# Attention 2: the low score pass as pairs of 64-row matmuls

## The chip, the core and the metric

The kernel runs on one core of one Trainium2 chip. The metric is device time in microseconds (us), the median of several runs. The engines are TensorE (PE in the profile, its weight loads PEld), VectorE (DVE), ScalarE (ACT), GpSimd (POOL) and SyncE (SP, which issues most transfers).

## What is computed

A trunk of two layers over 1024 frames of width 1024. Layer 1 mixes tokens by latent attention, layer 2 by differential attention; after each comes a SwiGLU block, and every step ends in a layer norm. The change concerns layer 2. Each of its 8 heads has two softmax maps of head width 64:

```python
logits = jnp.einsum('bqhmd,bkhmd->bmhqk', q_b, k) * scale
logits = logits - slopes[:, None, None] * dist
logits = jnp.where(_chunk_mask(i * Q_BLOCK, s), logits, NEG_BIG)
p = jax.nn.softmax(logits, axis=-1)
a = p[:, 0] - lam * p[:, 1]
o = jnp.einsum('bhqk,bkhe->bqhe', a, v)
```

The mask is causal over chunks of 64 frames, so a block of 128 queries with number i (0 to 7) sees (i + 1) * 128 keys.

## The kernel before, in words

Values in fp32 are split in two parts, a high part rounded to fp32r and a low part that is the rest, and a product is made of three matmuls: high by high, high by low, low by high. A tile planner orders the instructions of each engine ahead of time, by its own estimate of when operands and buffers are ready; at run time every engine works through its list in that order. `behind(i, j)` (line 167) tells the planner to keep instruction i after j.

**Attention 2** (from line 1263) works head by head. `proj_b` (line 1300) makes the queries and keys of a head, for half of the sequence at a time. A query tile `q2` has 1024 columns, 512 for each map; rows 0 to 63 and rows 64 to 127 both hold the map's high queries (a transfer copies them from one half of the partitions to the other). The keys `kt` hold, for map m, the high keys in the 64 rows from 64 * m and the low keys in the other 64. One matmul of 128 rows on `q2` and the keys so gives high by high plus high by low. The low queries `ql` of map m lie in the 64 rows from 64 * m, beside the high keys of that map; the other 64 rows are zero, so that a second matmul of 128 rows adds low by high alone. The zeros are written once: `store_zeros` (line 1233, in attention 1, slot 14) copies zeros to a tile and stores them to `zero_dr` (line 964), and six transfers at lines 1276 to 1279 load them into the three `ql` buffers. One of these three buffers is half of a tile that the profile calls `bq`; the other two are `ql`.

`score_b` (line 1329) scores one block of queries of one head: for each map it calls `softmax_block` (line 218). That takes the keys in one part up to 512 keys, else in two halves (widths 128, 256, 384, 512, then twice 320, 384, 448, 512). For each part it takes one PSUM bank of the group `s` (three of them in attention 2: `PS_BUFS_B`, line 38), runs the two matmuls into it (line 228), and lets VectorE add the bias, write the logits to SBUF and keep the extreme value (line 231, tiles `l_b` and `mx_b`). ScalarE then makes the exponentials with their sum (line 234), and VectorE the sum's reciprocal `r_b` (line 236). When both maps are done, GpSimd scales map 1 (line 1341), and VectorE combines the two (line 1342).

`attention` (line 270) sets the order: blocks are scored two ahead of the block that is transposed (`transpose_block`, tiles `pt_b`) and multiplied with the values (`pv_group`, tiles `o_b`); scores have the highest priority. The projections of the next head (`bp`), its values (`bv`), and the norms of finished heads (`norm_b2`, line 1368, which takes banks of the group `s` too) are put into numbered slots between the blocks.

Of the kernel before, what the change touches and what calls it, by code (L numbers as in the profile page):

```python
# [9 lines left out]
F32 = mybir.dt.float32  # L10
F32R = mybir.dt.float32r
AF = mybir.ActivationFunctionType
ALU = mybir.AluOpType
# [3 lines left out]
P = 128  # L17
# [17 lines left out]
BIGF = 3.0e38  # L35
# [7 lines left out]
def trunk(  # L43
# [32 lines left out]
    nc = tc.nc  # L76
    V, A, G, T = nc.vector, nc.scalar, nc.gpsimd, nc.tensor
# [9 lines left out]
    wp = ctx.enter_context(tc.tile_pool(name="wp", bufs=3))  # L87
# [12 lines left out]
    dr = ctx.enter_context(tc.tile_pool(name="dr", bufs=1, space=DRAM))  # L100
# [7 lines left out]
    def f32(t):  # L108
        return t.bitcast(F32)
# [4 lines left out]
    def ps_s(name):  # L114
        return ps.tile([P, 512], F32, tag="s", bufs=ps_bufs[0], name=name)
# [17 lines left out]
    def small(name, n=1):  # L133
        return sp.tile([P, 2], F32, tag="small", name=name, bufs=22)[:, :n]
# [32 lines left out]
    def behind(i, j):  # L167

        tc.add_manual_dep(
            i, j.name,  # L170
            mybir.DependencyInfo(mybir.DependencyClass.NoSync, mybir.DependencyReason.DATA),
            reason="kept in program order",
        )
# [44 lines left out]
    def softmax_block(lp, q_pass, s_bias, i, scale, name):  # L218
        n = (i + 1) * P
        nb = 1 if n <= 512 else 2  # L220
        w = n // nb
        l = lp.tile([P, 1024], F32, tag="l", name=f"l_{name}")
        mx = BIGF
        for b in range(nb):
            s = ps_s(f"s_{name}_{b}")
            ks = slice(b * w, (b + 1) * w)
            for j, (lh, rh) in enumerate(q_pass):
                T.matmul(s[:, :w], lh, rh[:, ks], start=(j == 0), stop=(j == len(q_pass) - 1))
            bv = s_bias[:, 896 - P * i + b * w:896 - P * i + (b + 1) * w]
            m = small(f"mx_{name}_{b}")  # L230
            V.tensor_tensor_reduce(l[:, ks], s[:, :w], bv, -scale, mx, ALU.add, ALU.min, m)  # L231
            mx = m
        sm = small(f"sm_{name}")
        newest["exp"] = A.activation(l[:, :n], l[:, :n], AF.Exp, bias=mx, scale=-1.0, accum_out=sm).ins  # L234
        r = small(f"r_{name}")
        V.reciprocal(r, sm)  # L236
        return l, r
# [32 lines left out]
    def attention(score, turn, mix, fill, la, hp):  # L270


        blocks = [(h, i) for h in range(H - 1) for i in range(NTB)] + [(H - 1, i) for i in LAST_ORDER]
        for fn in fill.get(-1, ()):
            fn()
        for b in range(la):
            score(*blocks[b])
        for b, (h, i) in enumerate(blocks):
            if b and i % 2 == 0:
                mix(blocks[b - 1][0], blocks[b - 1][1] // 2)  # L280
            if b + la < len(blocks):
                with tc.high_priority(hp[0]):
                    score(*blocks[b + la])
            with tc.high_priority(hp[1]):
                turn(h, i)
            for fn in fill.get(b, ()):
                fn()
        mix(blocks[-1][0], blocks[-1][1] // 2)
# [672 lines left out]
    spin(8, "spin0")  # L961

    o_dr = [[dr.tile([H, P, 256], F32, name=f"o_dr{l}_{g}") for g in range(4)] for l in range(2)]
    zero_dr = dr.tile([P, 512], F32, name="zero_dr")
    wo_dr = [dr.tile([P, 2, D], F32, name=f"wo_dr{h}") for h in range(H)]
    xs_dr = [dr.tile([S, D], F32, name=f"xs_dr{l}") for l in range(3)]

# [6 lines left out]
    ba, cos, sin = (krp.tile([P, S], F32, tag=t, name=t) for t in ("ba", "cos", "sin"))  # L974
# [130 lines left out]
    with ast as st:  # L1105
        pool = st.enter_context(tc.tile_pool(name="a1", bufs=2, reuse_waits="tile"))
        vp = st.enter_context(tc.tile_pool(name="a1v", bufs=12, side="right", reuse_waits="tile"))
        lp = st.enter_context(tc.tile_pool(name="a1l", bufs=4, side="right", reuse_waits="tile"))
# [97 lines left out]
        def at(slot, fn, *args):  # L1206
            fill.setdefault(slot, []).append(lambda: fn(*args))
# [9 lines left out]
        for h in range(1, H):  # L1217
            b = 8 * (h - 1)
# [11 lines left out]
        at(10, load_late)  # L1230
        at(12, make_late)

        def store_zeros():
            t = wp.tile([P, 1024], F32R, tag="wl", name="zeros")
            A.copy(t[:, :512], ba[:, :512])
            nc.sync.dma_start(zero_dr, f32(t[:, :512]))

        at(14, store_zeros)
        attention(score_a, turn_a, mix_a, fill, 2, (0, 0))

    banks("ps2", PS_BUFS)
# [22 lines left out]
    with ExitStack() as st:  # L1264
        lp = st.enter_context(tc.tile_pool(name="b1l", bufs=5, reuse_waits="tile"))
        pool = st.enter_context(tc.tile_pool(name="b1", bufs=2, reuse_waits="tile"))
        ptp = st.enter_context(tc.tile_pool(name="b1p", bufs=4, reuse_waits="tile"))
        bb = pool.tile([P, S], F32, tag="bb", name="bb", bufs=1)
# [4 lines left out]
        ob = big_tile("bo", F32)  # L1273
        q_hi = [qt[0][:, 0], qt[0][:, 1], qt[1][:, 0]]
        q_lo = [qt[1][:, 1]] + [pool.tile([P, S], F32R, tag=f"ql{j}", name=f"ql{j}", bufs=1) for j in range(2)]
        for ql in q_lo:
            for mp in range(2):
                b = slice(64 - mp * 64, 128 - mp * 64)
                nc.sync.dma_start(f32(ql[b, mp * 512:mp * 512 + 512]), zero_dr[b])

        def values_b(pr, tb):
            if ("v", pr) not in wts:
# [46 lines left out]
        def score_b(h, i):  # L1329
            c = slice((i % 4) * P, (i % 4) * P + P)  # L1330
            n = (i + 1) * P
            (q2, ql), k = q_slot[h, i // 4], kt[h % 2]
            (l0, r0), (l1, r1) = [
                softmax_block(
                    lp,
                    [(t[:, m * 512:m * 512 + 512][:, c], k[:, m]) for t in (q2, ql)],
                    bb, i, float(2.0 ** -(h + 1)), f"b{h}_{i}_{m}",
                )
                for m in range(2)
            ]  # L1340
            G.tensor_scalar(l1[:, :n], l1[:, :n], r1, nlam, ALU.mult, ALU.mult)  # L1341
            V.scalar_tensor_tensor(l0[:, :n], l0[:, :n], r0, l1[:, :n], ALU.mult, ALU.add)
            lt[h, i] = l0
# [67 lines left out]
        for h in range(1, H):  # L1411
            b = 8 * (h - 1)
# [20 lines left out]
        b = 8 * (H - 1) - 2  # L1433
        at(b - 1, begin_out)
        for slot, what, args in (
# [3 lines left out]
        ):  # L1439
            at(b + slot, lambda what, *a: getattr(proj[0], what)(*a), what, *args)  # L1440
        attention(score_b, turn_b, mix_b, fill, 2, (0, 60))
        norm_b(H - 1, 0, 2)
        norm_b2(H - 1, 0, 2)
# [94 lines left out]
```

## Time and profile before

| | |
|---|---|
| median of 3 runs | 2290.31 us (2287.85 to 2290.47) |
| the profiled execution | 2289.49 us |
| its span | 2287.7 us |
| granted clock of TensorE | 0.996 |
| first and last score of attention 2 | 1135.2 us, 1546.5 us |

The profile is of one execution. Times in its views are in microseconds from the start of the span, unless marked ns. "128*128 128x384" on a matmul is the size of the weights and of the result. A matmul's record runs from its start to a modelled end, and records of successive matmuls overlap; the time that a matmul takes of TensorE is read from the start of one to the start of the next. "idle before <- X" is the time in which an engine stood still before an instruction, and what it waited for.

### The profile page before, as it was taken

What the parts mean: (1) busy time and instruction counts of PE and PEld (TensorE: products, weight loads), DVE (VectorE), ACT (ScalarE), POOL (GpSimd) and SP (SyncE); (2) the same over time, 40 slices, a digit from 0 to 9 for tenths busy, and PEclk for the clock granted to TensorE, in tenths of its full rate; (3) what the DMA queues carried; (4) which work ended last, traced back from release to release, by engine and by line L of the source; (5) the groups of instructions that cost most, each with busy time, mean ns of one, the idle gap of its engine ahead of it and who ended that gap; (6) DMA issues with size and microseconds to landing.
All of it is one profiled execution on the core that took longest, in us unless ns stands there. A gap on an engine that the chain in (4) does not pass through costs nothing. (4 is left out here: it accounts for less than half of the span.)

```text
span 2287.7 us, 31159 instructions
## 1 busy us (share of the span) xinstructions
PE 2248.8 (98%) x11426; PEld 1916.5 (84%) x11426; DVE 1548.3 (68%) x2887; ACT 1019.3 (45%) x2101; POOL 871.6 (38%) x682
## 2 busy tenths in 40 slices
PE   9999999999999999999999999999999999999997
PEld 9888898888888887888888888987778888887886
DVE  6666765596666568667476666676586566657777
ACT  4465664352333334445465656555432233334353
POOL 2233452114444445555232424221014444436564
PEclk9999999999999999999999999999999999999999
DMA  6121325334313238554310212144344232337453
GB/s 205 41 94 56 123 97 184 135 141 141 126 69 138 73 117 328 187 185 166 107 47 24 65 38 70 37 194 129 120 161 157 69 123 85 122 129 306 141 203 123
DMA packets 104281, 289.33 MB, mean 126 GB/s; under 512 B 8640, under 2 KB 31808, under 8 KB 93632
## 3 DMA queue, kind: packets, MB, share of 16 engines
q1 hardware_dynamic: 100128, 277.90, 34.6%
q0 software_dynamic: 4000, 9.44, 1.4%
q8 instruction: 90, 1.47, 0.3%
q14 instruction: 63, 0.52, 0.1%
HBM read 205.78 MB, written 77.33 MB: 124 GB/s over the span
## 5 line engine op out<-in xcount | busy, mean ns | idle before, releaser
L513 ACT CAST op_g<-gr 128x512 fp32r<-128x512 f32 x240 | 147.5, 622 | 410.3 <-PE gb L557 227.7
L513 POOL TENSOR_TENSOR op_g<-gr,op_g 128x512 fp32r<-128x512 f32 x104 | 143.9, 1389 | 295.2 <-DVE tmp L650 154.0
L513 DVE TENSOR_TENSOR op_h<-rh,op_h 128x512 fp32r<-128x512 f32 x154 | 155.6, 1041 | 62.3 <-ACT op_h L513 62.3
L557 PE MATMUL ga<-xh_m,op_g 128*128 128x512 f32 x512 | 168.0, 389 | 0.0
L513 ACT CAST op_h<-rh 128x512 fp32r<-128x512 f32 x154 | 93.0, 620 | 155.3 <-PE dx L834 47.2
L834 PE MATMUL dw<-op_w_t,op_h 128*128 128x512 f32 x660 | 151.1, 390 | 0.0
L834 PEld LDWEIGHTS dw<-op_w_t,op_h 128*128 128x128 f32 x660 | 123.6, 188 | 25.7 <-DVE op_h L513 0.2
L234 ACT ACTIVATE l_b<-l_b,mx_b 128x256 f32<-128x256 f32 (+7 forms) x128 | 99.6, 778 | 78.4 <-DVE mx_b L231 75.5
L1341 POOL TENSOR_SCALAR l_b<-l_b,r_b,cst 128x128 f32<-128x128 f32 (+3 forms) x64 | 52.8, 825 | 205.9 <-DVE r_b L236 199.9
L834 PE MATMUL dx<-op_w_b,op_h 128*128 128x512 f32 x528 | 124.5, 397 | 5.3 <-DVE op_w_b L513 5.1
L513 POOL TENSOR_TENSOR op_w_t<-tt,op_w_t 128x512 fp32r<-128x512 f32 x66 | 98.4, 1493 | 79.7 <-ACT op_w_t L513 77.0
L834 PEld LDWEIGHTS dx<-op_w_b,op_h 128*128 128x128 f32 x528 | 101.1, 192 | 28.0 <-DVE op_w_b L513 6.0
L513 DVE TENSOR_TENSOR op_g<-gr,op_g 128x512 fp32r<-128x512 f32 x136 | 111.6, 822 | 9.5 <-ACT op_g L513 9.0
L557 PE MATMUL gb<-t4h_f,op_g 128*128 128x512 f32 x352 | 115.8, 390 | 0.6 <-DVE tmp L642 0.5
L557 PE MATMUL gc<-t1h_f,op_g 128*128 128x512 f32 x352 | 115.8, 389 | 0.5 <-ACT op_g L513 0.5
L557 PE MATMUL gb<-t3h_f,op_g 128*128 128x512 f32 x352 | 115.4, 389 | 0.7 <-ACT op_g L513 0.7
L557 PE MATMUL gc<-b22h_f,op_g 128*128 128x512 f32 x352 | 115.5, 389 | 0.0
L557 PE MATMUL gb<-t2h_f,op_g 128*128 128x512 f32 x352 | 114.8, 389 | 0.0
L557 PEld LDWEIGHTS ga<-xh_m,op_g 128*128 128x128 f32 x512 | 96.1, 188 | 20.0
L513 POOL TENSOR_TENSOR op_g<-s,op_g 128x512 fp32r<-128x512 f32 x40 | 55.4, 1385 | 149.2 <-ACT op_g L513 149.2
L155 PE MATMUL bp<-xT_f,h_wb 128*128 128x512 f32 x256 | 103.0, 402 | 0.0
L157 PE MATMUL bp<-xT_f,l_wb 128*128 128x512 f32 x256 | 101.6, 397 | 0.0
(376 smaller groups left out, 6751.8 us busy)
## 6 DMA issues: line engine op xcount, KB each, us to landing
gr<-in_w_gu SPq DMA_DIRECT2D x44, 1024.0 KB, 6.9
rh<-h_dr SPq DMA_DIRECT2D x28, 1024.0 KB, 5.3
h_dr<-sh SPq DMA_DIRECT2D x22, 1024.0 KB, 4.9
h_dr<-hp SPq DMA_DIRECT2D x22, 768.0 KB, 4.1
tt<-in_w_dn SPq DMA_DIRECT2D x22, 512.0 KB, 9.2
rh<-h_dr SPq DMA_DIRECT2D x14, 768.0 KB, 4.4
z<-xs_dr SPq DMA_DIRECT2D x16, 512.0 KB, 11.7
rw_b<-in_w_dn SPq DMA_DIRECT2D x8, 1024.0 KB, 8.3
```

What stands on the lines that cost most here:

```text
L155: T.matmul(ps_out, lh, rh, start=(i == 0), stop=False)
L157: T.matmul(ps_out, ll, rh, start=False, stop=(i == n - 1))
L234: newest["exp"] = A.activation(l[:, :n], l[:, :n], AF.Exp, bias=mx, scale=-1.0, accum_out=sm).ins
L513: return A.copy(hi, src).ins, eng.tensor_tensor(lo, src, f32(hi), ALU.subtract).ins
L557: T.matmul(o, w[:, a, kc], x[b][:, k, :], start=(first and k == 0 and (a, b) == (0, 0)), stop=(k == 3 and a == 1), skip_group_check=True,)
L834: T.matmul(o, h[:, a, c], w[:, b_], start=(first and (a, b_) == (0, 0)), stop=(last and a == 1), skip_group_check=True,)
L1341: G.tensor_scalar(l1[:, :n], l1[:, :n], r1, nlam, ALU.mult, ALU.mult)
```

## The change

`score_b` no longer calls `softmax_block`. For each part of the keys it takes two banks, one for each map, and issues the high matmuls of both maps (128 rows), then the low matmuls of both maps. A low matmul has 64 rows: those from 64 * m of the low queries and of the keys. A `behind` keeps the first low matmul after the second high one. VectorE's two reductions of the part follow, and when all parts are done, map 0's exponentials and reciprocal, then map 1's. The zeros are no longer needed: their copy, their store and their six loads are removed. What follows the softmax is unchanged.

```diff
-    zero_dr = dr.tile([P, 512], F32, name="zero_dr")
...
-        def store_zeros():
-            t = wp.tile([P, 1024], F32R, tag="wl", name="zeros")
-            A.copy(t[:, :512], ba[:, :512])
-            nc.sync.dma_start(zero_dr, f32(t[:, :512]))
-
-        at(14, store_zeros)
...
-        for ql in q_lo:
-            for mp in range(2):
-                b = slice(64 - mp * 64, 128 - mp * 64)
-                nc.sync.dma_start(f32(ql[b, mp * 512:mp * 512 + 512]), zero_dr[b])
...
             (q2, ql), k = q_slot[h, i // 4], kt[h % 2]
-            (l0, r0), (l1, r1) = [
-                softmax_block(
-                    lp,
-                    [(t[:, m * 512:m * 512 + 512][:, c], k[:, m]) for t in (q2, ql)],
-                    bb, i, float(2.0 ** -(h + 1)), f"b{h}_{i}_{m}",
-                )
-                for m in range(2)
-            ]
+            nb = 1 if n <= 512 else 2
+            w = n // nb
+            ls = [lp.tile([P, 1024], F32, tag="l", name=f"l_b{h}_{i}_{m}") for m in range(2)]
+            mx = [BIGF, BIGF]
+            for b in range(nb):
+                ks = slice(b * w, (b + 1) * w)
+                ss = [ps_s(f"s_b{h}_{i}_{m}_{b}") for m in range(2)]
+                pe = []
+                for t in (q2, ql):
+                    for m, s in enumerate(ss):
+                        a = slice(0, P) if t is q2 else slice(m * 64, m * 64 + 64)
+                        pe.append(T.matmul(
+                            s[:, :w], t[a, m * 512:m * 512 + 512][:, c], k[a, m, ks], start=(t is q2), stop=(t is ql),
+                            skip_group_check=True,
+                        ).ins)
+                behind(pe[2], pe[1])
+                bv = bb[:, 896 - P * i + b * w:896 - P * i + (b + 1) * w]
+                for m, s in enumerate(ss):
+                    x = small(f"mx_b{h}_{i}_{m}_{b}")
+                    V.tensor_tensor_reduce(
+                        ls[m][:, ks], s[:, :w], bv, -float(2.0 ** -(h + 1)), mx[m], ALU.add, ALU.min, x
+                    )
+                    mx[m] = x
+            rs = []
+            for m in range(2):
+                sm = small(f"sm_b{h}_{i}_{m}")
+                A.activation(ls[m][:, :n], ls[m][:, :n], AF.Exp, bias=mx[m], scale=-1.0, accum_out=sm)
+                r = small(f"r_b{h}_{i}_{m}")
+                V.reciprocal(r, sm)
+                rs.append(r)
+            (l0, l1), (r0, r1) = ls, rs
```

## Prediction

> **What bounds the kernel now.** I read the page's busy shares first, then the busy time of the second attention's stretch, then who waits there, and last the single matmuls in order of time.
>
> The page's first lines:
>
> ```profile
> span 2287.7 us, 31159 instructions
> ...
> PE 2248.8 (98%) x11426; PEld 1916.5 (84%) x11426; DVE 1548.3 (68%) x2887; ACT 1019.3 (45%) x2101; POOL 871.6 (38%) x682
> ```
>
> TensorE is busy for 98% of the span. Two stretches (start:end, length, then busy time and instructions of PE, PEld, DVE, ACT and POOL, the granted clock, DMA share, GB/s): that of the zeros' loads, and from the first score of attention 2 to nearly its end.
>
> ```profile
> 1068.00:1090.00 22.00, 22.00 (x123) 19.16 (x122) 15.09 (x30) 12.21 (x24) 7.43 (x5) 1.00 0.20 61
> 1135.00:1550.00 415.00, 411.35 (x2496) 363.98 (x2495) 283.25 (x847) 244.06 (x562) 131.70 (x126) 1.00 0.21 68
> ```
>
> In the second stretch TensorE is idle for 415.00 - 411.35 = 3.65 us, and VectorE, the next, is busy for 283 of 415. The waits of that stretch (who waits, for whom: total us, times, longest):
>
> ```profile
> DVE l_b L231 <- PE s_b L228: 23.0, 25, 4.1
> ...
> PE s_b L228 <- DVE mx_b L231: 1.5, 2, 1.1
> ```
>
> VectorE waits for scores more than TensorE waits for banks. A matmul that disappears here should therefore leave the span, as long as the row of work behind it can move up. Which matmuls are touched, by tile:
>
> ```profile
> L228 PE MATMUL s_b<-bk,bq x256: 220/358/741, 1135.2 to 1546.5; 128*128 128x384 f32 x32, 128*128 128x512 f32 x32, 128*128 128x320 f32 x20, 128*128 128x448 f32 x20
> L228 PE MATMUL s_b<-bk,ql x128: 272/340/486, 1150.1 to 1527.9; 128*128 128x384 f32 x32, 128*128 128x512 f32 x32, 128*128 128x320 f32 x24, 128*128 128x448 f32 x24
> ```
>
> Together 384, which is 96 groups of four: two maps, each with a high pass and a low pass. (One of the three low-query buffers lies in a bq tile, hence 256 and 128.) All are 128*128, full height. By the code a head has one group of width 128, one of 256, two of 320, three of 384, two of 448 and three of 512: 12 groups, times 8 heads.
>
> A matmul's record is longer than its place in the row, so I price by start to start. Runs of scores and what follows them:
>
> ```profile
> 1180.06 0.27 PE L228 MATMUL s_b<-bk,bq 128*128 128x128 f32 x1
> ...
> 1180.51 0.45 PE L155 MATMUL bp<-xT_f,h_wb 128*128 128x512 f32 x1
> ...
> 1260.35 0.33 PE L228 MATMUL s_b<-bk,bq 128*128 128x384 f32 x1
> ...
> 1261.04 0.39 PE L157 MATMUL bp<-xT_f,l_wb 128*128 128x512 f32 x1
> ...
> 1296.77 0.31 PE L228 MATMUL s_b<-bk,ql 128*128 128x320 f32 x1
> ...
> 1297.21 0.40 PE L156 MATMUL bp<-xT_f,h_wb 128*128 128x512 f32 x1
> ...
> 1337.19 0.28 PE L228 MATMUL s_b<-bk,bq 128*128 128x256 f32 x1
> ...
> 1337.67 0.27 PE L160 MATMUL pt_b<-ident,l_b 128*128 128x128 f32 x1
> ...
> 1343.20 0.40 PE L228 MATMUL s_b<-bk,ql 128*128 128x512 f32 x1
> 1343.43 0.39 PE L228 MATMUL s_b<-bk,bq 128*128 128x512 f32 x1
> ...
> 1343.89 0.27 PE L160 MATMUL pt_b<-ident,l_b 128*128 128x128 f32 x1
> ...
> 1425.62 0.36 PE L228 MATMUL s_b<-bk,ql 128*128 128x448 f32 x1
> 1425.82 0.36 PE L228 MATMUL s_b<-bk,bq 128*128 128x448 f32 x1
> ...
> 1426.63 0.39 PE L155 MATMUL bp<-xT_f,h_wb 128*128 128x512 f32 x1
> ```
>
> Four matmuls of 128 take 0.45 us, four of 384 0.69, three of 320 0.44, four of 256 0.48, three of 512 0.69, five of 448 1.01. One matmul's place s is then 0.1125, 0.1725, 0.147, 0.120, 0.230 and 0.202 us. Below 256 columns s falls no further: there the weight load sets the pace, so 0.1125 is one load's place. The loads of the last run:
>
> ```profile
> 1425.62 0.19 PEld L228 LDWEIGHTS s_b<-bk,bq 128*128 128x128 f32 x1
> 1425.82 0.19 PEld L228 LDWEIGHTS s_b<-bk,ql 128*128 128x128 f32 x1
> ```
>
> Each load starts just as the matmul ahead of its own starts (1425.62, 1425.82): one set of weights is prepared while another is in use.
>
> **The change part by part.**
>
> *The pair.* Each group's four matmuls stay four instructions with four loads, but the last two have 64 rows each, on the two halves of the array and into two banks. No row of this trace shows such a matmul. Its price lies between nothing beyond its neighbour (side by side) and its full place. I take side by side, because the halves share neither weights nor banks, and both are ready once the low queries are there. The loads I take one after the other, both from the start of the last high matmul, as the load rows suggest: 2 x 0.1125 = 0.225 must fit beside that matmul. A group then takes s + max(s, 0.225) + s, where it now takes 4s. Saved: 0.230 at 512, 0.808 - 0.629 = 0.179 at 448, 0.69 - 0.57 = 0.120 at 384, 0.588 - 0.519 = 0.069 at 320, 0.48 - 0.465 = 0.015 at 256, nothing at 128. Per head 3 x 0.230 + 2 x 0.179 + 3 x 0.120 + 2 x 0.069 + 0.015 = 1.561, for 8 heads 12.5 us. If the two half loads also run side by side, a whole s goes in every group: per head 0.690 + 0.404 + 0.5175 + 0.294 + 0.120 + 0.1125 = 2.138, in all 17.1 us.
>
> [...]
>
> *Changes of row count.* The row of matmuls now changes height twice a group, 192 times. The nearest rows are changes of another kind, from scores to a transpose: the two scores from 1343.43 to the transpose at 1343.89 have 0.23 us each, like those before them, so this change costs nothing. The other end is the overlap of one matmul's record with the next, 0.39 - 0.23 = 0.16 us. I take 0, by the row of the change, and give the other end to a rival.
>
> *Banks.* A group now takes two of the three score banks at once, where a map's block took one at a time. In blocks of 640 to 1024 keys (4 a head, 32 in all) the second half's second matmul needs the bank that the first half's map 0 leaves. The reduction that frees a bank (count | busy, mean ns):
>
> ```profile
> L231 DVE CUSTOM_DVE_ANT_0 l_b<-s_b,bb 128x512 f32<-128x512 f32 x32 | 21.7, 679 | 0.4 <-PE s_b L228 0.3
> ```
>
> Behind a score that waits stands everything else of TensorE (projections, values, transposes, products), and VectorE waits for all of those. The price lies between a gain of the 3.65 us that TensorE is idle and 32 x 0.679 = 21.7 us, if nothing stood between the halves. The planner orders the row by when it expects banks to be free and has most of TensorE's work to put between, so I stay near the present rows: the 1.5 us of waiting doubles, +1.5.
>
> *The exponentials.* Map 0's now comes behind both maps' reductions. GpSimd needs map 1's sum, which came last before too, and two blocks are scored ahead; I cost it at nothing. If that cover is gone, at the end of the last head, it is one reduction, 0.68 us.
>
> *The zeros.* Removed are one copy on ScalarE, one store and six loads of SP's queue:
>
> ```profile
> L1279 SPq DMA_DIRECT2D ql<-zero_dr x4: 444/517/598, 1079.3 to 1086.6; - x4
> L1279 SPq DMA_DIRECT2D bq<-zero_dr x2: 518/550/582, 1070.7 to 1071.3; - x2
> ```
>
> The loads are 4 x 0.517 + 2 x 0.550 = 3.2 us of issue on SP, ahead of transfers for the next weights. TensorE is busy throughout that stretch (22.00 of 22.00), so this gives nothing. The copy and its store are one instruction each in attention 1, where TensorE is the busiest engine as well (98% of the span); they give nothing either. The projection that writes the low queries loses its wait for the zeros, which no row shows on TensorE.
>
> *The sum.* The profiled execution took 2289.49 us, its span of 2287.7 and 1.8 around it: 2289.49 - 12.5 + 1.5 = 2278.5. It lies 0.8 below the median of the three runs, 2290.31, so the forecast on that scale is 2279.3. What a measurement of this kernel can tell from no change is about 0.2%, 4.6 us: faster means below 2285.7, slower above 2294.9.
>
> **The rivals.**
>
> *The array empties at each change of height.* Then the overlap between records is lost 192 times: 192 x 0.16 = 30.7 us, and the time is 2279.3 + 30.7 = 2310.0, slower. It decides above 11.0 / 192 = 0.057 us a change; from 0.081 us on, the kernel is measurably slower. For it: the trace has no change of height, so nothing excludes it. Against it: other changes of kind cost nothing. [...]
>
> *The second half's load waits for the first half's matmul to start.* Each load row starts with the matmul ahead, and the second half's matmul has the first half's ahead of it. The pair then takes s + 0.1125, and a group saves s - 0.1125: per head 3 x 0.1175 + 2 x 0.0895 + 3 x 0.060 + 2 x 0.0345 + 0.0075 = 0.788, in all 6.3 us, with the banks 2285.5.
>
> *The change doesn't do what it says.* The halves run one after the other, or the planner parts them. Nothing is saved, the banks cost 1.5: 2291.8, and more if the bank waits go towards their upper end. For it: a score waits for a bank even now (the 1.5 us), and a planner that fills such a wait can fill it between the halves. Against it: both halves become ready together.
>
> **How the numbers follow.** The forecast has 0.38 (faster 0.37, within 0.01). The emptying array has 0.37: nothing in the trace bears on it directly, and prices between 0.057 and 0.081 give about no change (slower 0.31, within 0.06). The late load has 0.13, on the bound (faster 0.06, within 0.07). No overlap has 0.12 (within 0.07, slower 0.05). That is 0.43 faster, 0.21 within, 0.36 slower. The forecast's own range is 2273 to 2284: below, loads side by side and no bank wait (2290.3 - 17.1); above, bank waits some 5 us larger. The whole range, 2273 to 2311, takes in the emptying array at its full price; what is left out, about 0.15, is an array that also loses its prepared weights, or banks at their upper end.
>
> **What would show it.** Right: the two low matmuls of a pair start within some 0.01 us of each other and the next matmul about s later; TensorE's idle time before scores that wait for mx_b stays at about 3 us, twice the 1.5; the stretch of attention 2 is 11 us shorter. The emptying array would show as a first low matmul, and a first full one behind the pair, that start later than s after the one before, by the same amount at every width. The late load would show as low matmuls 0.11 us apart at every width, no overlap as low matmuls a whole s apart. Bank waits would show in the waits row, mx_b before s_b. My forecast is wrong if the starts around the pair leave gaps of over 0.057 us each.

## The result and the profile after

The changed kernel takes 2329.42 us, the median of 4 runs (2323.9 to 2330.81), beside 2289.88 for the kernel before: 39.5 us or 1.73% slower, ratio 1.0173 with a 95% interval of 1.0161 to 1.0185. The prediction was 2279.3 with a range of 2273 to 2311: the side was wrong, and the range did not hold the time. The profiled execution took 2328.64 us, its span 2326.9.

The page's first lines:

```profile
span 2326.9 us, 31150 instructions
...
PE 2281.4 (98%) x11426; PEld 1908.5 (82%) x11426; DVE 1553.8 (67%) x2887; ACT 1013.0 (44%) x2100; POOL 872.4 (37%) x682
```

The number of matmuls is the same, and TensorE is still busy for 98%; the share says nothing. Where the time came in is seen from the ends of the stages: the first score of attention 2 starts at 1134.9 us (1135.2 before), the last at 1586.6 (1546.5 before). All of it lies in attention 2. Its stretch, with the columns of the windows shown before, and its waits:

```profile
1135.00:1587.00 452.00, 441.13 (x2468) 353.70 (x2466) 286.51 (x837) 237.01 (x555) 132.11 (x125) 0.98 0.19 61
```

```profile
DVE l_b L1341 <- PE s_b L1333: 55.2, 45, 6.4
...
PEld s_b L1333 <- issue: 28.2, 113, 0.4
...
PEld s_b L1333 <- DVE mx_b L1341: 12.4, 15, 2.2
...
PE s_b L1333 <- DVE mx_b L1341: 8.4, 9, 2.0
```

Three things differ from before. TensorE is idle for 452.00 - 441.13 = 10.9 us (3.65 before), 8.4 of it before scores that wait for a bank (1.5 before). The granted clock is 0.98 (1.00 before). And a row stands high that was 1.0 us in 4 times before: the weight loads of scores stood still 113 times for 28.2 us, waiting for nothing that the profile shows. What this is can be read from single instructions, first the matmuls of a group of width 512, then the loads at the same time:

```profile
1301.31 0.29 PE L267 MATMUL o_b<-pth_b,bvh 128*128 128x256 f32 x1
1301.43 0.40 PE L1333 MATMUL s_b<-bk,bq 128*128 128x512 f32 x1
1301.76 0.50 PE L1333 MATMUL s_b<-bk,ql 64*128 64x512 f32 x2
1302.18 0.39 PE L267 MATMUL o_b<-ptl_b,bvh 128*128 128x256 f32 x1
1302.41 0.28 PE L267 MATMUL o_b<-pth_b,bvl 128*128 128x256 f32 x1
```

```profile
1301.31 0.19 PEld L1333 LDWEIGHTS s_b<-bk,bq 128*128 128x128 f32 x1
1301.76 0.19 PEld L1333 LDWEIGHTS s_b<-bk,ql 64*128 64x128 f32 x2 [0.26 <-issue]
1302.18 0.19 PEld L267 LDWEIGHTS o_b<-ptl_b,bvh 128*128 128x128 f32 x1 [0.24 <-issue]
```

The row "64*128 ... x2" holds both low matmuls of the pair: they do run side by side, and so do their loads; in all 88 pairs that stand together the two starts lie 3 to 4 ns apart. But the full-height matmul ahead has a place of 1301.76 - 1301.43 = 0.33 us in place of 0.23, the pair one of 0.42, and the 256-wide matmul behind it 0.23 in place of 0.12. At each change of height the next load starts not with the matmul ahead but later: that of the pair at 1301.76, 0.1 us after the usual place of the matmul ahead is over (1301.43 + 0.23), with no load running in the 0.26 us before it. The load then lies bare, since its matmul is recorded as starting with it (1301.76 and 1301.76, 1302.18 and 1302.18). Behind the pair that costs the 256-wide matmul 0.23 - 0.12 = 0.11 us. The pair's place is 0.19 us too long; taken with the same 0.11 us for its own bare load, an estimate, some 0.1 us is left ahead of the change back, as ahead of the pair.

### The profile page after: what moved, and what is told of

It reads as the page before. It is cut to its first block, busy times and chain, and to the rows that moved or that the text cites. A ratio compares the mean times of both kernels' runs of the same rounds, so it can differ in the third digit from the quotient of the medians.

```text
span 2326.9 us, 31150 instructions
## 1 busy us (share of the span) xinstructions
PE 2281.4 (98%) x11426; PEld 1908.5 (82%) x11426; DVE 1553.8 (67%) x2887; ACT 1013.0 (44%) x2100; POOL 872.4 (37%) x682
## 5 line engine op out<-in xcount | busy, mean ns | idle before, releaser
L155 PE MATMUL bp<-xT_f,h_wb 128*128 128x512 f32 x256 | 102.4, 400 | 0.0
L156 PE MATMUL bp<-xT_f,h_wb 128*128 128x512 f32 x256 | 101.5, 397 | 0.0
```

What stands on the lines that cost most here:

```text
L155: T.matmul(ps_out, lh, rh, start=(i == 0), stop=False)
L156: T.matmul(ps_out, lh, rl, start=False, stop=False)
```

## The experiments

**Full height in the new order.** The changed kernel with the zeros back (the removed lines of the diff), and

```diff
-                        a = slice(0, P) if t is q2 else slice(m * 64, m * 64 + 64)
+                        a = slice(0, P)
```

> The changed kernel with the zeros back and the low matmuls at 128 rows: the new order and the two banks at once stay, the change of height goes. Theory (each change of height empties the array and lays a weight load bare, about 0.21 us a change by the starts in the changed kernel's trace): the height costs about 33 us, the order and the banks the rest, so 2293 to 2300. Rival (the banks and the order cost most of the 39 us): 2315 or more. Rival (a half-height matmul is slow in itself): as by the theory.

Measured: 2308.02 us, 20.1 above the kernel before, measured beside it (ratio 1.0086, 1.0071 to 1.0101). Between the two theories: the order and the banks cost 20 us, the height the other half. The waits and the windows of half clock (the three last numbers of a window are clock, DMA share and GB/s):

```profile
DVE l_b L1352 <- PE s_b L1344: 38.7, 30, 5.7
...
PEld s_b L1344 <- DVE mx_b L1352: 14.9, 17, 2.3
...
PE s_b L1344 <- DVE mx_b L1352: 10.6, 10, 2.1
```

```profile
1189.00:1192.40 3.40, 2.88 (x13) 2.86 (x14) 3.22 (x11) 2.35 (x9) 1.70 (x2) 0.50 0.19 39
1236.80:1243.60 6.80, 6.23 (x22) 4.98 (x22) 6.15 (x23) 4.56 (x16) 1.79 (x4) 0.50 0.00 0
1352.90:1356.30 3.40, 3.15 (x12) 2.67 (x13) 2.75 (x10) 1.46 (x5) 0.53 (x2) 0.50 0.01 2
1468.90:1472.30 3.40, 3.40 (x13) 2.94 (x13) 2.75 (x13) 2.60 (x9) 0.55 (x1) 0.50 0.00 0
```

The row of stalled loads ("issue") is gone from the top, the bank waits are not: 10.6 us. And in 17.0 us the clock was half (0.50), so by estimate some 8.5 us of TensorE's time went. That is 9.1 more bank wait and 8.5 of clock, most of the 20.1.

**Single low matmuls at half height, in the old order.** The kernel before without zeros, its pass list made

```diff
-                    [(t[:, m * 512:m * 512 + 512][:, c], k[:, m]) for t in (q2, ql)],
+                    [
+                        (t[a, m * 512:m * 512 + 512][:, c], k[a, m])
+                        for t, a in ((q2, slice(0, P)), (ql, slice(m * 64, m * 64 + 64)))
+                    ],
```

> The kernel before, map by map as it was, with each low matmul at 64 rows by itself and no zeros: 192 half-height matmuls, 384 changes of height, no pairs. Theory: 384 x 0.21 = 81 us and no place saved, about 2370. Rival (a half-height matmul is slow in itself, 192 of them as in the changed kernel, 0.21 us each): about 2330. Rival (banks and order): the kernel before, 2290.

Measured: 2356.8 us, 68.9 above the kernel before (ratio 1.0299, 1.0284 to 1.0314). The price of half-height matmuls in themselves (2330) falls, the price of changes stands, at 68.9 / 384 = 0.18 us a change, a little below the 0.21 read from the starts. The stretch of attention 2 and one of its matmuls:

```profile
1134.00:1613.00 479.00, 478.17 (x2477) 362.40 (x2475) 286.06 (x836) 243.26 (x557) 130.12 (x125) 1.00 0.18 58
```

```profile
1300.31 0.39 PE L228 MATMUL s_b<-bk,bq 128*128 128x512 f32 x1
1300.63 0.49 PE L228 MATMUL s_b<-bk,ql 64*128 64x512 f32 x1
1301.05 0.50 PE L157 MATMUL bp<-xT_f,l_wb 128*128 128x512 f32 x1
1301.39 0.39 PE L155 MATMUL bp<-xT_f,h_wb 128*128 128x512 f32 x1
```

Hardly any idle time (0.8 us) and full clock, so this run shows the changes alone: places of 0.32, 0.42 and 0.34 us where 0.23 is usual. The single low matmul takes 0.42, just what the pair took in the changed kernel: by these rows the second of a pair cost nothing.

**All three products at half height.** In the changed kernel, three pairs in place of two full matmuls and a pair:

```diff
-                for t in (q2, ql):
+                for j, t in enumerate((q2, ql, ql)):
                     for m, s in enumerate(ss):
-                        a = slice(0, P) if t is q2 else slice(m * 64, m * 64 + 64)
+                        a = slice(m * 64, m * 64 + 64)
...
-                behind(pe[2], pe[1])
```

> The changed kernel with all three products as pairs of 64-row matmuls (in place of high by low, low by high is added once more, since that lies on the same rows): 96 visits and 192 changes as in the changed kernel, but 576 half-height matmuls in place of 192. Theory (the cost is of the change): three places a group as before, so 2325 to 2335. Rival (the cost is of each half-height matmul, 0.21 us): 384 more, about 2410.

Measured: 2380.62 us (ratio 1.0405, 1.0387 to 1.0422), between the two. The run did not do what it was to do: the planner, here without `behind`, parted the pairs, and the trace has 193 visits of the half height in place of 96, and 78 pairs side by side. Recounted, 386 changes at 0.18 are 69 us, and 576 - 78 = 498 places in place of 384 are 114 x 0.178 = 20 us: 2288 + 89 = 2377. That comes near, but it was worked out afterwards and leaves out a term: attention 2 has 20.4 us at half clock here, which cost some 10 us more (2387). The run tells little of the price. Its stretch and those windows:

```profile
1132.00:1641.00 509.00, 506.33 (x2679) 383.66 (x2679) 299.00 (x849) 242.75 (x564) 131.37 (x126) 0.98 0.17 55
1247.00:1250.40 3.40, 3.40 (x18) 3.40 (x17) 0.92 (x5) 0.72 (x4) 0.56 (x1) 0.51 0.00 0
1270.90:1274.30 3.40, 3.40 (x16) 3.12 (x16) 1.50 (x7) 2.12 (x5) 0.10 (x1) 0.51 0.00 0
1298.20:1305.00 6.80, 6.80 (x25) 4.74 (x24) 4.44 (x6) 2.66 (x5) 2.37 (x1) 0.50 0.28 72
1434.80:1441.60 6.80, 6.80 (x23) 4.94 (x25) 4.26 (x6) 1.69 (x3) 2.37 (x1) 0.50 0.28 86
```

**No low product.** The changed kernel with the two high matmuls of a group alone (the low by high product is left out):

```diff
-                pe = []
-                for t in (q2, ql):
...
-                behind(pe[2], pe[1])
+                for m, s in enumerate(ss):
+                    T.matmul(s[:, :w], q2[:, m * 512:m * 512 + 512][:, c], k[:, m, ks], start=True, stop=True)
```

> The changed kernel without the low by high product: only the two full-height matmuls of a group, in the new order with the two banks at once. It tests what a matmul that goes is worth here. If TensorE's row sets the time, 192 places of 0.178 us (mean over the widths) go against the full-height kernel of this call: 34 us less than it, about 2263. If banks or VectorE take over, less goes: 2280 or more.

Measured: 2270.73 us (ratio 0.9923, 0.9908 to 0.9938), 37.3 below the full-height run; of these, 3.4 us are half clock that this run has less of (10.2 us of it in attention 2 against 17.0). The rest is the 34 expected: a matmul that went was worth its place here, 0.178 us in the mean, and the premise of the prediction holds.

**Pairs kept together.** The low pair of the changed kernel at a higher priority:

```diff
-                for t in (q2, ql):
-                    for m, s in enumerate(ss):
+                for t, hp in ((q2, 0), (ql, 400)):
+                    with tc.high_priority(hp):
+                        for m, s in enumerate(ss):
...
```

> The changed kernel with a higher priority in the planner for the low pair, so that nothing is put between its two matmuls (8 of its 96 pairs were parted, which gave 104 visits of the half height in place of 96). Theory (a change of height costs about 0.18 us, from the 384 changes of the kernel with single half-height matmuls): 16 changes and 8 places of 0.178 fewer, about 4 us less than the changed kernel: 2325. If parted pairs do not matter: 2329.

Measured: 2323.63 us (ratio 1.015, 1.0134 to 1.0165), some 6 us less than the changed kernel, which was measured at another time. All 96 pairs are together now. But the clock loses only some 5 us in attention 2 in place of 10, so the drop cannot be put down to the parted pairs alone.

**Four score banks.** The changed kernel, and its full-height control, with

```diff
-PS_BUFS_B = (3, 2, 2, 1)
+PS_BUFS_B = (4, 2, 1, 1)
...
+                if (tb, heads[0], nh) == (LAST_ORDER[1], self.HEADS, 1):
+                    where = ps_o
```

> The changed kernel with four score banks in place of three; the bank comes from the transposes, which keep one (and one late product of the output projection takes the bank of the value products). Theory (of the 39 us some 19 come from waiting for score banks: 7 us more idle time, and 10 us of clock that was lost in the windows of half clock behind those waits): these go, the changes of height stay, about 2311. Rival (the new order of the exponentials, not the banks): 2329 as before. Above it, if the single transpose bank makes waits of its own.

> The same four score banks with the low matmuls at full height on zeros: the control for the run with four banks. Theory: neither bank waits nor changes of height, so about the kernel before, 2288 to 2294; the run with four banks and pairs should lie about 21 us above it, as it did with three. Rival (order of the exponentials): 2308, as with three banks.

Measured: 2377.03 us with pairs (ratio 1.0382, 1.0365 to 1.0399), 2351.91 at full height (1.0273, 1.0258 to 1.0289). Both are far slower, so this was no cure. The control's stretch and waits:

```profile
1135.00:1600.00 465.00, 436.48 (x2451) 375.16 (x2450) 288.52 (x830) 239.01 (x551) 130.20 (x125) 0.95 0.19 61
```

```profile
PE s_b L1346 <- DVE mx_b L1354: 14.1, 19, 1.7
...
PE pt_b L160 <- DVE ptl_b L256: 6.4, 8, 1.9
```

The transposes now wait for their one bank, and the scores wait for theirs as before; the clock falls to 0.95. The pairs still lie 25.1 us above the control, near what the theory of changes had (21). Whether four banks would do without taking one from the transposes stays open: no run here had more than the eight banks of these two versions (3 + 2 + 2 + 1 and 4 + 2 + 1 + 1).

**One visit a block, with four banks.** First all four high matmuls of a block of two halves, then its two low pairs:

```diff
+            ss = [[ps_s(f"s_b{h}_{i}_{m}_{b}") for m in range(2)] for b in range(nb)]
...
+            for t in (q2, ql):
+                for b in range(nb):
+                    for m in range(2):
...
+            behind(pe[2 * nb], pe[2 * nb - 1])
...
```

> Four score banks, and in blocks of two halves first all four high matmuls and then the two low pairs one behind the other: 64 visits of the half height in place of 96 to 104. Theory: 64 x 2 x 0.18 = 23 us for the changes less 17 us for the saved places, some 6 us above the full-height control, about 2296, if banks do not run out. Rival: a block now takes all four banks at once, bank waits and half clock come back, 2310 or more.

Measured: 2387.09 us (ratio 1.0428, 1.0413 to 1.0444). The rival came true: in the 496.00 us of its attention 2 TensorE is idle for 20.8 us, 10.4 of them before scores that wait for a bank, at a mean clock of 0.93. And the visits did not fall: the planner parted the pairs into 129 visits.

**One bank at a time, full height.** The full-height version of the changed kernel, each map's matmuls and reduction in turn:

```diff
...
+                for m in range(2):
+                    s = ps_s(f"s_b{h}_{i}_{m}_{b}")
+                    for t in (q2, ql):
+                        T.matmul(s[:, :w], t[:, m * 512:m * 512 + 512][:, c], k[:, m, ks], start=(t is q2), stop=(t is ql))
...
```

> The full-height version of the changed kernel (2308 us), but with each map's two matmuls and its reduction in turn, so that a part takes one score bank at a time as in the kernel before; the halves of the keys stay outside, the maps inside, and both exponentials come at the end. Theory (the 20 us of the new order come from taking two of three banks at once): 2288 to 2294. Rival (they come from the order of the halves and from the later exponentials): about 2308.

Measured: 2284.91 us, the median of 10 runs (ratio 0.9985, 0.9976 to 0.9995): 23.1 below the run that takes both banks first. It even lies 0.15% below the kernel before, which is less than the 0.2% that the prediction took as measurable; ten runs make the interval narrow. Its stretch and waits:

```profile
1135.00:1545.00 410.00, 406.90 (x2481) 361.12 (x2480) 289.03 (x846) 239.37 (x561) 132.81 (x126) 1.00 0.22 68
```

```profile
PE s_b L1343 <- DVE mx_b L1345: 1.7, 2, 1.4
```

The bank waits are back at 1.7 us and the clock at 1.00. Halves outside, maps inside, and both exponentials at the end cost nothing; taking two banks at once does, together with what goes with it here: both high matmuls ahead of both low ones, held there by `behind`, and the two reductions behind all four. These were not tried apart; that banks run short is seen in the waits.

**Half the dose of changes.** The kernel before, with map 0's low matmul alone at 64 rows:

```diff
-                    [(t[:, m * 512:m * 512 + 512][:, c], k[:, m]) for t in (q2, ql)],
+                    [
+                        (t[a, m * 512:m * 512 + 512][:, c], k[a, m])
+                        for t, a in ((q2, slice(0, P)), (ql, slice(0, 64) if m == 0 else slice(0, P)))
+                    ],
```

> The kernel before, with the low matmul of map 0 alone at 64 rows: 96 half-height matmuls, 192 changes of height, half of those of the kernel with single half-height matmuls (which lay 69 us above the kernel before, 0.18 us a change), in the old order of banks. Theory (a price for each change): 34 us above the kernel before, about 2324. Rival (a price for having the half height at all, or one that saturates): far from half of 69 us.

Measured: 2322.52 us (ratio 1.0153, 1.0138 to 1.0168), 34.3 above the kernel before: half of 68.9, and again 34.3 / 192 = 0.18 us a change (0.17 without one window of 3.4 us at half clock in the profiled attention 2).

## Why the prediction was wrong

*The pair: right.* The halves ran side by side, their starts 3 to 4 ns apart; the pair's place of 0.42 us is that of one low matmul. So a pair saves a whole place, as in the upper of the two estimates (17.1), not the 12.5 of the forecast. That the loads follow one another from the start of the last high matmul was wrong both ways: the two half loads start together, but only 0.1 us after that matmul's usual place is over. The 0.1125 us taken for a load's place is near what the loads of the 128-wide scores show before (1180.00, 1180.11, 1180.22 and 1180.33 us), where four matmuls take 0.45 us beside 0.48 at 256; that the load sets this pace was read from these rows, not tried apart.

*Changes of row count: the step that failed.* "I take 0, by the row of the change": a change from scores to transposes is one of the kind of matmul at the same height, and said nothing of a change of height. Measured, a change costs 0.18 us, at two doses and in the old order of banks. The prediction's own point of decision was 0.057. The changed kernel has 104 visits, so 208 x 0.18 = 37.4 us; its 88 pairs that stayed together save 88 x 0.178 = 15.7. The step is +21.8 us in place of -12.5. The price is nearly the same at every width, as the rival's sign asked: by the starts in the run with single low matmuls, where nothing waits and with the places of the prediction, it is 0.19 to 0.21 us a change at widths from 256 to 512, and 0.16 at 128.

The rival of the emptying array had the sign, and with 0.16 us nearly the price, by taking the overlap of two records for it. The starts show it made otherwise, of some 0.1 us beyond the usual place before the next load starts and some 0.1 us of a bare load (the rows at 1301.31 to 1302.41). Whether the array empties in that time, no row shows.

*Banks: mis-sized.* Forecast +1.5 us, measured 20.1 by the full-height run in the new order, and gone in the run that takes one bank at a time. That scores would wait for a bank was named; the value near the present rows was the wrong choice. The upper end, 21.7, comes near 20.1 by luck: it was a price of waits alone, and 8.5 of the 20.1 are half clock, a term that the prediction does not have. It also looked for the waits in the second halves of blocks of 640 to 1024 keys. In the changed kernel the four longest, 6.6 of the 8.4 us, stand before blocks of 256, which have one part. One place shows how a wait arises (VectorE in order, in the changed kernel):

```profile
1192.18 0.68 DVE L1306 SCALAR_TENSOR_TENSOR ql<-bp,bq 64x512 fp32r<-64x512 f32 x1
1192.79 0.40 DVE L1363 COPY bo<-o_b 128x256 f32<-128x256 f32 x1
1193.12 0.14 DVE L1350 RECIPROCAL r_b<-sm_b 128x1 f32<-128x1 f32 x1
1193.19 0.40 DVE L256 TENSOR_TENSOR ptl_b<-pt_b,pth_b 128x256 fp32r<-128x256 f32 x1
1194.30 0.17 DVE L1350 RECIPROCAL r_b<-sm_b 128x1 f32<-128x1 f32 x1 [0.71 <-ACT l_b L1348]
1194.38 0.27 DVE L1341 CUSTOM_DVE_ANT_0 l_b<-s_b,bb 128x128 f32<-128x128 f32 x1
```

```profile
1192.32 0.39 PE L1333 MATMUL s_b<-bk,bq 128*128 128x256 f32 x1
1194.71 0.38 PE L1333 MATMUL s_b<-bk,bq 128*128 128x256 f32 x1 [2.01 <-DVE mx_b L1341]
...
1243.38 0.58 PE L1333 MATMUL s_b<-bk,bq 128*128 128x256 f32 x1 [1.90 <-DVE mx_b L1341]
...
1364.01 0.38 PE L1333 MATMUL s_b<-bk,bq 128*128 128x256 f32 x1 [1.36 <-DVE mx_b L1341]
...
1484.24 0.39 PE L1333 MATMUL s_b<-bk,bq 128*128 128x256 f32 x1 [1.36 <-DVE mx_b L1341]
```

Two banks hold the scores of a 128-wide block, whose reduction stands in VectorE's list behind four other things and a reciprocal that waits for ScalarE. The next block has got one bank at 1192.32 and needs a second; all of TensorE's list stands behind that matmul for 2.01 us. VectorE is busy for only 286.51 of the 452 us of the stretch, and still the order of its list sets when a bank comes free.

*Exponentials and zeros: right.* The run with one bank at a time has the new order of exponentials and loses nothing. The doses of 384 changes without zeros and 192 with them give the same price per change, so the zeros were worth nothing that shows (each time is known to some 3 us).

*The sum.* +21.8 for height and +20.1 for banks are 41.9 us; measured were 39.5. The trace of the changed kernel divides it alike: attention 2 is 40.4 us longer from its first score to its last, 7.2 of them more idle time and some 10 half clock, which leaves some 23 for height. The range ended at 2311 because it took in one of the two prices in full, not both. What the prediction named as left out, at about 0.15, is near what came: an array that also loses its prepared weights, and banks at their upper end, but both at once.

## What to carry to other kernels

In this kernel the row of full-height matmuls paid 2 x 0.18 us for each visit of half-height ones (2 x 0.16 at width 128), while a pair side by side saved one place, 0.1125 us at 128 and 0.23 at 512: so a pair alone between full-height matmuls lost at every width from 128 to 512, and the zeros were the cheaper way, 20.1 us above the kernel before in the new order where the pairs were 39.5. Before two things are made adjacent, count the buffers that they hold at once, and look in the consumer's list, not at its busy share, for when it gives them back. A range should hold the case in which two separate prices both come.

## What was not expected of the hardware

The granted clock of TensorE was 0.50 in stretches behind the waits. In the changed kernel the windows are these:

```profile
1195.20:1198.60 3.40, 3.40 (x16) 3.19 (x17) 3.37 (x12) 1.90 (x9) 1.51 (x3) 0.50 0.19 39
1243.00:1249.80 6.80, 6.42 (x20) 4.16 (x20) 6.07 (x25) 4.50 (x17) 2.19 (x3) 0.50 0.00 0
1365.90:1369.30 3.40, 3.08 (x13) 2.59 (x13) 2.75 (x11) 1.54 (x7) 0.55 (x1) 0.50 0.00 0
1485.30:1492.10 6.80, 6.36 (x23) 4.68 (x23) 6.14 (x22) 3.86 (x14) 1.66 (x3) 0.50 0.00 0
```

20.4 us at half clock cost an estimated 10 us (half of them), as much again as the waits. What half clock does to a place is seen in the run with all three products at half height, inside its window from 1298.20: the 256-wide matmuls of the values start 0.21 us apart there (1300.80 to 1302.93), where 0.12 is usual. The first window comes after two waits of 1.39 and 2.01 us within 5 us; no single wait of the stretch was longer. Over the full-height kernels it goes with the idle time: none in attention 2 with 3 to 4 us of idle time (the kernel before, one bank at a time), 8.5 us lost in the full-height run with 14, some 22 (44.2 us of its 465 at half clock) in the four-bank control with 28. But waits are not all of it. The run with all three products at half height was idle for 2.7 of 509.00 us, and still had the four windows shown there: TensorE was busy through all of them, and no gap in the 7 us ahead of one was over 0.1 us. The run with single low matmuls, with about as many changes of height (384 beside 386), had none. So what halves the clock stays open, and that the waits did it in the changed kernel is argued, not shown.
